# Two MLPs and two attentions on one core: third sweep in groups of two pairs, second attention run without MLP steps inside, low parts of a weight kept in DRAM, a reordered norm chain

## The chip, the cores and the metric

The kernel runs on one core of one Trainium2 chip. The metric is device time of the whole program, from the first to the last instruction and a little around them, as the median of several runs.

## What is computed

A decoder trunk of two layers on one sequence of 1024 tokens, width 1024, all in float32. Layer 0 mixes with an mLSTM in chunks of 128; layer 1 with a causal attention of 8 heads, whose keys and values come from a shared low-rank latent. Each mixer and each MLP stands between two RMS norms:

```python
x = x + g1 * rmsnorm(mixer(modulate(rmsnorm(x, norm_g[l, 0]), sh1, sc1)), norm_g[l, 1])
h = modulate(rmsnorm(x, norm_g[l, 2]), sh2, sc2)
x = x + g2 * rmsnorm(jnp.square(jax.nn.relu(h @ mlp_w1[l])) @ mlp_w2[l], norm_g[l, 3])
```

The shifts, scales and gates come from `silu(c) @ ada_w[l] + ada_b[l]`. The MLP's hidden width is 4096, so `mlp_w1` is 1024 x 4096 and `mlp_w2` 4096 x 1024.

## The kernel before

**Numbers.** A float32 product is made of three matmuls (`mm3`, L244 to L246): every operand is split into a high part (`fp32r`, a cast on ScalarE) and a low part (the difference, on VectorE). A weight of 128 x 1024 is loaded into `raw` (4 buffers), cast to `wh` (L202) and subtracted to `wl` (L203), both in a ring of 8 (`ws`). A weight's `load` stands two steps ahead of its use (`AHEAD`).

**Halves and sweeps.** The sequence is worked on as two halves of 512 tokens, `hfs[0]` and `hfs[1]`. A layer's MLP runs over both in three sweeps. Hidden columns are taken in 16 pairs (p, 16 + p) of 128 columns. Sweep 1 makes the first 16 hidden blocks of half 0, sweep 2 the other 16, and both use seven products for eight (a scheme with sums and differences of the halves' inputs and of weight blocks), whose remainders are kept in DRAM: `m` (sweep 1's partial product), `u` (two sums per pair) and `s` (a weight sum). Sweep 3 (`third`, L1014) makes the hidden blocks of half 1 from `s` and `u`. A sweep is a list of steps: `hid` steps, each 24 matmuls of 128 x 512 (36 in sweep 2) that make hidden blocks, and `out` steps (`up_cols` in layer 0, `up_rows` in layer 1), which multiply the group's hidden blocks by `mlp_w2` into PSUM (`pm`) and add the result to the running sum in SBUF (`accumulate`, the `L211 DVE k<-k,pm` rows). A group is 1, 2 or 4 pairs; the `out` steps of a group follow the `hid` steps of the next one. The second weights are loaded and split again in sweep 3.

After a `hid`'s matmuls come an addition on VectorE, two functions on ScalarE (relu, square; L928, L929), a cast (L457) and a subtraction (L458).

**Two streams.** `two_streams(dense, other, fill)` (L2342) writes the order on TensorE by hand: `other`, a mixer, yields a number n after each piece of work, and n steps of `dense`, the MLP, are put behind it, 0.5 for each stretch that `dense` yields (a `yield "within"` splits a step). `fill` (the `ada` vectors) is advanced beside them. So layer 0's sweep 3 runs beside the first half's latents, attention, output projection and norm (`mixer1(hfs[0], ..)`); layer 1's sweep 1 beside those of the second half (`mixer1(hfs[1], ..)`). Sweep 2 of layer 1 needs what the second half's norm gives (`ops`), so the MLP steps that are left when the attention is done are what TensorE has beside the projection (`wout`), the residual and the norm chain (`post`, L2235). A scheduler then orders every engine's list, TensorE's given order kept, by a model of the times and by priorities (`prompt`, `tc.high_priority`).

**Second attention.** Half 1 attends to all keys: 8 heads, two units each (j = 2, 3) of two 128-query blocks, on 640 to 1024 keys. A unit is: scores (`score_mm`, L1498 to L1504, into both banks of a `pm`), softmax (L1508 maximum, L1509, L1510 exponential, L1511, L1512 scaling), `turned` (transpositions on TensorE, L1614 and L1625, each with a cast and a subtraction) in rounds of four key blocks, and `products`. The loop (`attend`, L1603) does, in each round, the last round's products, the transpositions, after the last round the next unit's scores, then MLP steps by `next(dense)`, here `cycle((0, 0.5))`.

**Norm chain.** `post` scales eight blocks of 128 x 512 by the norm (L2261), then forms from them and from half 0's stored `keep` (`u`) the operands of sweep 2: `ops[2]`, `ops[3]`, later `ops[4]`; `aside` forms `ops[0]` and `ops[1]` for sweep 3. Sweep 2's own weights need five differences on VectorE for each `hid` (L980 to L987, the first result used is `wv`, L985).

## Time and profile before

| | |
|---|---|
| median of 3 runs | 2411.64 us (2410.61 to 2415.65) |
| the profiled execution | 2413.85 us, its span 2412.1 us |
| TensorE (PE) busy | 2286.9 us, 95% of the span |
| weight loads (PEld), VectorE (DVE), ScalarE (ACT) | 78%, 73%, 45% |
| mean granted TensorE clock | 0.978 |
| moved | 448.47 MB, mean 186 GB/s |

PEclk is the granted TensorE clock as a share of full speed. In a group's row stand the line, the engine, the operation, output and inputs by name, shapes, the count, then busy us and the mean in ns, then the idle time before them and what ended it. A wait's row reads: who, waited for whom, us in total, times, the longest.

### The profile page before, as it was taken

Reading aid. Unit: us, or ns where it says so; the run is one execution under the profiler, and the core shown is the slowest. Engines: PE = TensorE matmul, PEld = TensorE weight load, DVE = VectorE, ACT = ScalarE, POOL = GpSimd, SP = SyncE. Lnnn points to the kernel's source line nnn. Section 1 sums busy time; section 2 is a strip of 40 time slices with the busy share of each in tenths; the row PEclk is TensorE's granted clock in tenths of the full one; section 3 lists DMA queues with packets and bytes.
Section 4 is the critical chain, followed back from the end, with each engine's and each line's share of the span. In section 5 each row is a group of like instructions: output and inputs, shape, how many; then the busy total and the mean of one; then the engine's idle time right before and its main releaser. Section 6 shows DMA issues by size and latency. Waiting matters only on the chain. (4 is left out here: it accounts for less than half of the span.)

```text
span 2412.1 us, 31013 instructions
## 1 busy us (share of the span) xinstructions
PE 2286.9 (95%) x11274; PEld 1891.3 (78%) x11274; DVE 1756.6 (73%) x2825; ACT 1075.7 (45%) x1795; POOL 18.3 (1%) x95
## 2 busy tenths in 40 slices
PE   8999999999999889899989999999999699999998
PEld 6888888888778677777878777788877488878887
DVE  6666767799787777788875987766647876666556
ACT  4365336565323245344444465444444333454433
POOL 1000000000000000000000000000000000000000
PEclk9999999999999999999999999999999899999999
DMA  9544555556697875545554664965256487675321
GB/s 316 172 128 123 157 149 164 178 187 207 211 290 224 248 263 167 161 130 176 170 171 146 205 217 150 308 207 183 90 153 206 127 272 234 217 259 196 117 88 70
DMA packets 384186, 448.47 MB, mean 186 GB/s; under 512 B 28867, under 2 KB 258304, under 8 KB 384032
## 3 DMA queue, kind: packets, MB, share of 16 engines
q1 hardware_dynamic: 383744, 446.38, 58.2%
q8 instruction: 89, 1.46, 0.2%
q14 instruction: 65, 0.53, 0.1%
q0 software_dynamic: 288, 0.10, 0.0%
HBM read 341.55 MB, written 104.86 MB: 185 GB/s over the span
## 5 line engine op out<-in xcount | busy, mean ns | idle before, releaser
L202 ACT CAST wh<-raw 128x1024 fp32r<-128x1024 f32 (+2 forms) x339 | 344.3, 1018 | 513.7 <-PE ps L244 119.5
L203 DVE TENSOR_TENSOR wl<-raw,wh 128x1024 fp32r<-128x1024 f32 (+2 forms) x339 | 400.0, 1182 | 223.7 <-ACT wh L202 210.7
L244 PE MATMUL ps<-k,wl 128*128 128x512 f32 x1100 | 437.7, 398 | 9.3 <-DVE wl L203 4.4
L245 PE MATMUL ps<-k,wh 128*128 128x512 f32 x1100 | 432.1, 393 | 2.5 <-DVE k L458 2.4
L246 PE MATMUL ps<-k,wh 128*128 128x512 f32 x1100 | 430.9, 392 | 0.0
L244 PEld LDWEIGHTS ps<-k,wl 128*128 128x128 f32 x1100 | 208.1, 189 | 57.3 <-DVE wl L203 5.4
L245 PEld LDWEIGHTS ps<-k,wh 128*128 128x128 f32 x1100 | 208.3, 189 | 46.9 <-DVE k L458 4.8
L246 PEld LDWEIGHTS ps<-k,wh 128*128 128x128 f32 x1100 | 208.2, 189 | 44.1
L211 DVE TENSOR_TENSOR k<-k,pm 128x512 f32<-128x512 f32 (+1 forms) x234 | 200.7, 884 | 57.0 <-PE pm L246 56.4
L244 PE MATMUL pm<-hd,wl 128*128 128x512 f32 x512 | 205.2, 401 | 5.7 <-DVE k L211 5.7
L245 PE MATMUL pm<-hd,wh 128*128 128x512 f32 x512 | 201.7, 394 | 1.7 <-DVE hd L458 1.7
L246 PE MATMUL pm<-hd,wh 128*128 128x512 f32 x512 | 201.4, 393 | 0.0
L244 PE MATMUL pm<-wh,hd 128*128 128x512 f32 x488 | 193.2, 396 | 6.6 <-DVE hd L458 2.7
L245 PE MATMUL pm<-wl,hd 128*128 128x512 f32 x488 | 190.8, 391 | 0.0
L246 PE MATMUL pm<-wh,hd 128*128 128x512 f32 x488 | 190.8, 391 | 0.0
L348 DVE SCALAR_TENSOR_TENSOR tma<-raw,cond,tma 128x512 f32<-128x512 f32 x168 | 125.7, 748 | 17.5 <-DMA raw<-in_ada_w_dram 9.1
L928 ACT ACTIVATE tmp<-tmp 128x512 f32<-128x512 f32 x80 | 50.5, 631 | 160.6 <-DVE tmp L211 136.2
L244 PEld LDWEIGHTS pm<-hd,wl 128*128 128x128 f32 x512 | 97.7, 191 | 28.4 <-DVE k L211 7.2
L245 PEld LDWEIGHTS pm<-hd,wh 128*128 128x128 f32 x512 | 97.7, 191 | 23.0 <-DVE hd L458 2.6
L244 PEld LDWEIGHTS pm<-wh,hd 128*128 128x128 f32 x488 | 92.0, 189 | 28.3 <-DVE hd L458 3.5
L246 PEld LDWEIGHTS pm<-hd,wh 128*128 128x128 f32 x512 | 97.4, 190 | 20.8
L246 PEld LDWEIGHTS pm<-wh,hd 128*128 128x128 f32 x488 | 92.0, 189 | 19.5
(425 smaller groups left out, 4324.0 us busy)
## 6 DMA issues: line engine op xcount, KB each, us to landing
raw<-in_mlp_w_dram SPq DMA_DIRECT2D x160, 512.0 KB, 4.7
raw<-in_ada_w_dram SPq DMA_DIRECT2D x80, 512.0 KB, 4.5
raw<-in_mlp_w_dram SPq DMA_DIRECT2D x128, 256.0 KB, 4.0
raw<-in_a_w_in_dram SPq DMA_DIRECT2D x44, 512.0 KB, 4.6
s<-k SPq DMA_DIRECT2D x32, 512.0 KB, 3.4
u<-k SPq DMA_DIRECT2D x32, 512.0 KB, 4.2
raw<-s SPq DMA_DIRECT2D x32, 512.0 KB, 3.4
xs<-k SPq DMA_DIRECT2D x40, 256.0 KB, 4.8
```

The source lines that it names most:

```text
L202: nc.scalar.copy(hi[:, :n], r[:, :n])
L203: i = nc.vector.tensor_sub(lo[:, :n], r[:, :n], hi[:, :n].bitcast(F32))
L211: return f(*a, **k)
L244: nc.tensor.matmul(o, ll, rh, start=start, stop=False)
L245: nc.tensor.matmul(o, lh, rl, start=False, stop=False)
L246: pe_last[0] = nc.tensor.matmul(o, lh, rh, start=False, stop=stop)
L348: nc.vector.scalar_tensor_tensor(acc, r[:, kk], cond[:, k : k + 1], acc, ALU.mult, ALU.add)
L928: nc.scalar.activation(s, s, AF.Relu)
```

## The change

- Layer 0's sweep 3 takes groups of two pairs (`[2] * 8` for `[1] * 14 + [2]`), layer 0's sweep 1 and layer 1's sweep 1 groups of four. With `own`, a group's `out` steps follow its own `hid` steps.
- `out` steps multiply the hidden blocks in the order in which they were made, both banks of `pm` side by side.
- In layer 0's sweeps 1 and 2 the low part of each second weight is also stored to DRAM (`lo`); sweep 3 loads it into the `ws` ring and does not subtract.
- `attend` has a branch for the second half: "group" first runs MLP steps to the end of a group, then scores of the next unit stand between a unit's transpositions, and MLP steps stand only behind the whole attention. The first half's MLP step per unit stands in one place.
- `two_streams` counts a step as 1 (or half at "within") and carries a remainder.
- `wout` in the mixers loads two weights ahead; `post` forms the difference of the two halves' blocks before the norm is known (eight scalings on ScalarE), and the rest of the old chain (`rest`) is put into sweep 2's `hid` steps 1 to 4. The yields after the second attention change.

```diff
--- before
+++ after
...
@@ -852,10 +855,16 @@
-    def wout(w, o, store, wide=False):
-
+    def wout(w, o, store, wide=False, ahead=0):
+
+        load = lambda m: wload([(0, 0, wcols(w, m * P))], P)
+        ready = [load(m) for m in range(ahead)]
+        if ahead:
+            yield
         for m in range(KD):
-            pt = proj_fm(w, m * P, o, one_pm if wide and m % 2 else ps)
+            if m + ahead < KD:
+                ready.append(load(m + ahead))
+            pt = proj_of(ready.pop(0), o, one_pm if wide and m % 2 else ps)
@@ -920,6 +929,7 @@
             self.keep = scratch([D, H], f"keep{l}")
+            self.lo = scratch([4, P, DFF // P, 256], f"lo{l}")
@@ -998,6 +1008,8 @@
                 prompt(nc.vector.tensor_add)(u2, u2, pt)
+                if p_ and ops["later"]:
+                    ops["later"].pop(0)()
@@ -1101,15 +1113,20 @@
             def out(ws):
-                for t in range(t0, t1):
-                    if t % 2 == 0:
-                        if t > t0:
-                            yield "within"
-                        b2 = pm()
-                    block(b2[:, t % 2], ws, t)
-                    if t % 2:
+                made = list(hids)
+                for t in range(t0, t1, 2):
+                    if t > t0:
+                        yield "within"
+                    b2 = pm()
+                    for j, q in enumerate(sorted(range(G), key=lambda q: made.index(fs[q]))):
+                        w, (hh, hl) = ws[q // 2], hids[fs[q]]
                         for e in range(2):
-                            self.accumulate((half, t - 1 + e, g), y.t[t - 1 + e][:, g], b2[:, e])
+                            mm3(
+                                b2[:, e], hh[:, ts(t + e, P)], hl[:, ts(t + e, P)],
+                                w[0][:, q % 2], w[1][:, q % 2], j == 0, j == G - 1,
+                            )
+                    for e in range(2):
+                        self.accumulate((half, t + e, g), y.t[t + e][:, g], b2[:, e])
@@ -1118,22 +1135,43 @@
             def out(w):
-                for m in range(i * n, (i + 1) * n):
-                    if m % 2 == 0:
-                        if m > i * n:
-                            yield "within"
-                        b2 = pm()
-                    pt = b2[:, m % 2]
-                    for q, f in enumerate(fs):
-                        c_ = ts(m - i * n, P)
-                        mm3(pt, w[0][:, q, c_], w[1][:, q, c_], *hids[f], q == 0, q == G - 1)
-                    if m % 2:
-                        self.accumulate((half, m), y.t[m // 2], b2)
+                for m in range(i * n, (i + 1) * n, 2):
+                    if m > i * n:
+                        yield "within"
+                    b2, made = pm(), list(hids)
+                    for j, q in enumerate(sorted(range(G), key=lambda q: made.index(fs[q]))):
+                        for e in range(2):
+                            c_ = ts(m + e - i * n, P)
+                            mm3(
+                                b2[:, e], w[0][:, q, c_], w[1][:, q, c_], *hids[fs[q]],
+                                j == 0, j == G - 1,
+                            )
+                    self.accumulate((half, m + 1), y.t[m // 2], b2)
             views = [(a, 0, wcols(w2, i * n * P, n * P, f, r)) for a, f, r in self.runs(fs)]
-            return lambda: wload(views, n * P), out
-
-        def steps(self, half, y, sweep, groups, prev=(), lead=False):
+
+            def load():
+                if not half:
+                    w = wload(views, n * P)
+                    nc.sync.dma_start(self.lo[i][:, fs[0] : fs[0] + G], w[1].bitcast(F32))
+                    return w
+                r = raw()
+                w = [
+                    sb.tile([P, 1024], F32R, tag="ws", bufs=WS, name=f"wk_{next(uid)}").rearrange(
+                        "p (a b) -> p a b", b=n * P
+                    )
+                    for _ in range(2)
+                ]
+                rv = r.rearrange("p (a b) -> p a b", b=n * P)
+                for a, f, k in self.runs(fs):
+                    nc.sync.dma_start(rv[:, a : a + k], wcols(w2, i * n * P, n * P, f, k))
+                    nc.sync.dma_start(w[1][:, a : a + k].bitcast(F32), self.lo[i][:, f : f + k])
+                nc.scalar.copy(w[0], rv)
+                return w
+
+            return prompt(load), out
+
+        def steps(self, half, y, sweep, groups, prev=(), lead=False, own=False):
@@ -1149,6 +1187,8 @@
                 prev = [self.up(half, y, fs, j, sweep == 3 and fs[-1] == 2 * NPR - 1) for j in range(len(fs))]
+                if own:
+                    steps, prev = steps + prev, []
@@ -1162,7 +1202,8 @@
                     yield from f(w)
-                    yield steps[(n - AHEAD + 1) % len(steps)][1].__name__
+                    after = steps[(n - AHEAD + 1) % len(steps)][1].__name__
+                    yield "lead" if (f.__name__, after) == ("out", "hid") else after
@@ -1172,9 +1213,9 @@
-        def sweep1(self, hf, y, sizes):
+        def sweep1(self, hf, y, sizes, own=False):
             g = self.groups(sizes, list, lambda p_: self.first(p_, hf.h2))
-            return self.steps(0, y, 1, g)
+            return self.steps(0, y, 1, g, own=own)
@@ -1196,12 +1237,12 @@
-        def sweep3(self, hf, y, sizes, buf):
+        def sweep3(self, hf, y, sizes, buf, own=False):
             )
-            steps, last = self.steps(1, y, 3, g)
+            steps, last = self.steps(1, y, 3, g, own=own)
@@ -1656,6 +1688,39 @@
+        def score(u, e):
+            st, n = pm(), (2 * u.j + e + 1) * P
+            score_mm(lambda g: st[:, g], hf.kk, u.q, u.kn, 2 * u.j + e)
+            u.prs.append(raw())
+            softmax(st.rearrange("p a b -> p (a b)")[:, :n], u.prs[e], n, e == 0)
+
+        def ahead():
+            for head, j in next(groups, []):
+                u = Half()
+                (u.hh, u.q, u.kn, u.v), u.j, u.nk, u.prs = head, j, 2 * j + 2, []
+                return u
+
+        if hf.i:
+            yield "group"
+            u = ahead()
+            for e in range(2):
+                score(u, e)
+            while u:
+                then, done = ahead(), []
+                for e in range(2):
+                    b0 = 4 * e
+                    work = [(u, b0, min(4, u.nk - b0))]
+                    done.append((work, turned(work)))
+                    if then:
+                        score(then, e)
+                    elif e:
+                        behind()
+                for work in done:
+                    products(*work)
+                yield next(dense)
+                u = then
+            return
+
@@ -1777,7 +1842,7 @@
         yield 0.5
-        yield from attend(hf, units(), cycle((0.5,)), lambda: load_o(hf), 0.5, piece)
+        yield from attend(hf, units(), cycle((1,)), lambda: load_o(hf), 0, piece)
@@ -1802,7 +1867,7 @@
-        yield from attend(hf, units(), cycle((0, 0.5)), lambda: load_o(hf))
+        yield from attend(hf, units(), cycle((0,)), lambda: load_o(hf))
@@ -2243,7 +2308,12 @@
                 )
-            u = FH(tiles=u)
+            u, d = FH(tiles=u), [k4v(), k4v()]
+            d = [d[k // 2][:, k % 2] for k in range(4)]
+            for k in range(4):
+                for j in (k, 4 + k):
+                    nc.scalar.activation(y[j], y[j], AF.Identity, scale=A[:, j : j + 1])
+                nc.vector.tensor_sub(d[k], y[4 + k], y[k])
@@ -2252,28 +2322,31 @@
         ops = hf.ops
-        ops[2], ops[3] = half_op(), half_op()
-        ts2 = []
+        ops[2] = half_op()
+        b1, b2 = ([sh[:, j : j + 1] for j in range(i, i + 4)] for i in (0, 4))
+        for k in range(4):
+            with tc.high_priority(PRIO):
+                nc.vector.tensor_mul(d[k], d[k], rstd)
+                nc.vector.scalar_tensor_tensor(d[k], d[k], b2[k], u[k], ALU.add, ALU.add)
+                split_mod(ops[2].hi[k], ops[2].lo[k], d[k], None)
+            yield waits[4]
+        ops[3] = half_op()
             with paced():
-                y1, y2, b = y[k], y[4 + k], sh[:, 4 + k : 5 + k]
-                for j in (k, 4 + k):
-                    nc.vector.scalar_tensor_tensor(
-                        y[j], y[j], A[:, j : j + 1], rstd, ALU.mult, ALU.mult
-                    )
-                nc.vector.tensor_sub(y1, y1, u[k])
                 t = tmc()
-                nc.vector.scalar_tensor_tensor(t, y2, b, y1, ALU.add, ALU.subtract)
-                split_mod(ops[2].hi[k], ops[2].lo[k], t, None)
-                ts2.append(t)
-            yield waits[4]
-        for k, t in enumerate(ts2):
-            with paced():
-                b1, b = sh[:, k : k + 1], sh[:, 4 + k : 5 + k]
-                nc.vector.scalar_tensor_tensor(u[k], t, b1, u[k], ALU.subtract, ALU.subtract)
-                split_mod(ops[3].hi[k], ops[3].lo[k], u[k], None)
-                nc.vector.scalar_tensor_tensor(u[4 + k], u[4 + k], b, t, ALU.add, ALU.subtract)
+                nc.vector.scalar_tensor_tensor(t, d[k], b1[k], u[k], ALU.subtract, ALU.subtract)
+                split_mod(ops[3].hi[k], ops[3].lo[k], t, None)
+                nc.vector.scalar_tensor_tensor(
+                    u[4 + k], u[4 + k], b2[k], d[k], ALU.add, ALU.subtract
+                )
             yield waits[5]
+
+        def rest(k):
+            nc.vector.tensor_mul(y[k], y[k], rstd)
+            nc.vector.tensor_sub(y[k], y[k], u[k])
+            nc.vector.tensor_mul(y[4 + k], y[4 + k], rstd)
+
+        ops["later"] = [lambda k=k: rest(k) for k in range(4)]
@@ -2343,7 +2416,7 @@
         traced = nc.cur_bb.bb.instructions
-        at, per = ["hid"], 0
+        at, per, due = "hid", 0, 0
@@ -2351,15 +2424,18 @@
                 per, n = more, 0
-            while n == "align" and at[0] != "hid" or n != "align" and n > 0:
-                at[0] = go(dense)
-                if at[0] is end:
+            whole = n in ("align", "group")
+            if not whole:
+                due = due + n if n else 0
+            while at not in ("lead", n == "align" and "hid") if whole else due > 0:
+                was, at = at, go(dense)
+                if at is end:
                 pace[0] = next(i for i in reversed(traced) if i.engine == dve)
-                if at[0] != "within":
+                if at != "within":
                     some(fill, per)
-                if n != "align":
-                    n -= 0.5
+                if not whole:
+                    due -= 0.5 if "within" in (was, at) else 1
@@ -2400,7 +2476,7 @@
-    steps, tail = ms[0].sweep1(hfs[0], z0, [4, 4, 4, 2, 2])
+    steps, tail = ms[0].sweep1(hfs[0], z0, [4] * 4)
@@ -2423,17 +2499,24 @@
         y = FH(claim=True)
+        last = wout(b_w_out[0], hf.o, lambda m, pt: evac(y[m], pt), ahead=2)
+        next(last)
         yield 1
-        yield "align"
-        for _ in wout(b_w_out[0], hf.o, lambda m, pt: evac(y[m], pt)):
+        if not hf.i:
+            yield "align"
+        for _ in last:
         yield from post(
-            hf, y, B2, x_cols, A3, adac(1, SH2), ms[1], ((3, 3, 3, 5, 1), (2, 1, 1, 4, 0.5, 0))[hf.i]
+            hf, y, B2, x_cols, A3, adac(1, SH2), ms[1], ((3, 3, 3, 5, 1), (2, 2, 2, 3, 0.5, 0.5))[hf.i]
+    turn_of = cycle((0, 1))
+
+        if next(turn_of):
+            return tmc(), tmp()
@@ -2442,12 +2525,12 @@
     two_streams(
-        ms[0].run(ms[0].sweep3(hfs[1], z1, [1] * 14 + [2], pair_buf)),
+        ms[0].run(ms[0].sweep3(hfs[1], z1, [2] * 8, pair_buf, True)),
     u0 = FH(claim=True)
-    steps, tail = ms[1].sweep1(hfs[0], u0, [2] * 8)
+    steps, tail = ms[1].sweep1(hfs[0], u0, [4] * 4, True)
...
```

`proj_of` multiplies a loaded weight as `proj_fm` did; the first half's `scores` keeps the shape for j < 2 alone.

More of the change, by code (lines that the diff above doesn't have):

```diff
@@ L1519, in scores @@
         prs = []
[L1520 to L1536 removed]
+        st = pm()
+        pr = raw().rearrange("p (a b) -> p a b", b=512)
+        for e in range(2):
+            score_mm(lambda g: st[:, e], kk, q, kn, 2 * j + e)
+        for e in range(2):
+            n = (2 * j + e + 1) * P
+            softmax(st[:, e, :n], pr[:, e], n, e == 0)
+            prs.append(pr[:, e])
         return prs
@@ L1657, in begin @@
             return us
+        def score(u, e):
[11 more added lines that the diff above has]
+            u = ahead()
+            for e in range(2):
+                score(u, e)
+            while u:
+                then, done = ahead(), []
+                for e in range(2):
+                    b0 = 4 * e
[10 more added lines that the diff above has]
+            return
         late = None
```

22 lines of the change are left out of this document (3 added, 19 removed).

## The prediction

> **What bounds the kernel now.** I read the busy time by stage first (VectorE is DVE, ScalarE ACT, TensorE PE, its weight loads PEld), then who PE waits for, then the chain that ended last at the worst place.
>
> ```profile
> core 0: us, PE busy (x) PEld busy (x) DVE busy (x) ACT busy (x) POOL busy (x), PEclk, DMA share, GB/s
> 0.00:445.00 445.00, 434.49 (x2693) 365.79 (x2694) 307.67 (x617) 208.22 (x422) 9.27 (x43) 1.00 0.56 172
> 445.00:640.00 195.00, 193.27 (x852) 158.23 (x851) 165.22 (x234) 107.70 (x152) 0.00 (x0) 1.00 0.63 199
> 640.00:880.00 240.00, 215.51 (x917) 174.29 (x916) 197.14 (x299) 78.21 (x110) 0.39 (x4) 0.96 0.81 250
> 880.00:1355.00 475.00, 443.08 (x2103) 364.99 (x2102) 361.98 (x578) 211.23 (x363) 4.04 (x20) 0.96 0.54 170
> 1355.00:1555.00 200.00, 186.45 (x806) 150.55 (x805) 160.48 (x228) 106.11 (x168) 0.76 (x5) 0.96 0.64 207
> 1555.00:1757.00 202.00, 195.51 (x1172) 169.46 (x1171) 136.46 (x239) 94.70 (x173) 3.23 (x17) 0.99 0.51 173
> 1757.00:1880.00 123.00, 119.51 (x521) 98.39 (x522) 76.27 (x104) 51.98 (x74) 0.20 (x2) 0.97 0.55 171
> 1880.00:1930.00 50.00, 26.98 (x106) 20.05 (x105) 44.76 (x71) 15.69 (x24) 0.00 (x0) 0.83 0.46 138
> 1930.00:2115.00 185.00, 185.00 (x837) 152.49 (x836) 124.13 (x181) 71.98 (x102) 0.39 (x4) 1.00 0.76 238
> 2115.00:2412.10 297.10, 287.13 (x1280) 237.09 (x1279) 182.45 (x282) 129.83 (x210) 0.00 (x0) 0.99 0.44 146
> ```
>
> The stages are: layer 0's mixer (to 445), its sweeps 1 and 2 (to 640 and 880), sweep 3 beside the first attention (to 1355), layer 1's sweep 1 beside latent work (to 1555), beside the second attention (to 1757), and beside output projection and norm (to 1930), then layer 1's sweeps 2 and 3. PE is the bound throughout. The change removes no matmul, so all it can win is PE idleness (stage length less PE busy) and half-rate clock (stage times one less PEclk). In 880:1355 that is 31.9 us idle and 19 us of clock, 51 together. In 640:880 it is 24.5 and 10; in 1757:1930, 26.5 and 12 (partly the same moments).
>
> The Trainium skill (Perfetto Trace Analysis, Identifying the Most-Contended Engine) calls matmul occupancy a poor measure of headroom and wants weight-load occupancy instead. In 880:1355 that would leave 110 us. The trace disagrees here: in 1930:2115 PE is never idle and PEld is still 82%.
>
> The timeline gives PE's pace; PE's waits and the busy time around the longest of them follow.
>
> ```profile
> 2300.74 0.39 PE L244 MATMUL ps<-k,wl 128*128 128x512 f32 x1
> ...
> 2305.50 0.39 PE L244 MATMUL ps<-k,wl 128*128 128x512 f32 x1
> ```
>
> These two rows are 21 matmuls apart: 0.227 us each, so an MLP step of 24 matmuls takes 5.45 us.
>
> ```profile
> PE ps L244 <- DVE wv L985: 18.8, 1, 18.8
> ```
>
> ```profile
> 1889.40:1908.20 18.80, 0.04 (x2) 0.03 (x1) 18.80 (x32) 6.78 (x11) 0.00 (x0) 0.64 0.02 10
> 1908.20:1912.00 3.80, 3.80 (x9) 3.00 (x10) 2.79 (x3) 2.66 (x5) 0.00 (x0) 0.53 0.99 294
> ```
>
> PE stood 18.8 us while DVE was busy in every one of them, and afterwards ran at about half rate.
>
> **The change, part by part.** I count savings as negative.
>
> *A, norm chain and cover of layer 1 (1757:1930).*
>
> ```profile
> 1877.35 3.40 DVE k L2261 x5
> ...
> 1907.52 0.60 DVE wv L985
> ```
>
> From the norm's result (1877.35) to the first `wv` (1907.52) DVE ran 30.2 us, 48 instructions by the chain's rows between these, 0.63 us each. In the changed program DVE's order has 56 there: the combination moves ahead of the norm, but the scheduler pulls eight products and four differences of the deferred `rest` forward into this stretch. That is 35 us, 5 more. PE's order, on the other hand, has five MLP steps after the norm's sum matmul instead of three, 10.9 us more cover. The 18.8 us would shrink to about 13; the longer yields before it (2, 2, 2, 3 for 2, 1, 1, 4) should take the other 7.7 us of idleness, and some clock. I take -12. If DVE eats the cover, 0; if everything goes, 26.5 and a little clock, -28.
>
> *B, second attention without MLP steps (1555:1757).*
>
> ```profile
> L458 DVE TENSOR_TENSOR hd<-pc,hd 128x512 fp32r<-128x512 f32 x47 | 31.8, 687 | 7.1 <-ACT hd L457 4.7 <-PE ps L245 1.7 <-issue 0.5
> ...
> L1508 DVE TENSOR_REDUCE sm<-pm 128x1 f32<-128x1024 f32 x7 | 8.5, 1220 | 2.1 <-PE pm L1504 2.1
> ...
> L1512 DVE TENSOR_SCALAR raw<-raw,sm 128x1024 f32<-128x1024 f32 x7 | 5.3, 752 | 0.2
> ...
> L1511 DVE RECIPROCAL sm<-sm 128x1 f32<-128x1 f32 x28 | 4.5, 162 | 15.4 <-ACT raw L1510 14.8
> ...
> L1509 DVE TENSOR_SCALAR sm<-sm 128x1 f32<-128x1 f32 x28 | 4.2, 150 | 0.5
> ```
>
> On ACT, and four of a unit's transpositions twice over in the chain:
>
> ```profile
> L1510 ACT ACTIVATE raw<-pm,sm 128x1024 f32<-128x1024 f32 x7 | 7.8, 1121 | 12.2 <-DVE sm L1509 12.2
> ...
> L1510 ACT ACTIVATION_READ_ACCUMULATOR raw<-pm,sm 128x1 f32 x28 | 5.4, 194 | 0.0
> ```
>
> ```profile
> 1742.13 0.87 PE pc L1614 x8
> ```
>
> The steps are moved, not removed: the code now runs whole groups until two of the four are done before the attention, and has 15 steps' worth of yields after it. Inside, PE's cover must come from the next unit's scores. A unit (two 128-query blocks of a head; 16 units) has a softmax chain after its last score of 1.22 + 0.15 + 1.12 + 0.19 + 0.16 + 0.75 = 3.6 us at 1024 keys. PE's order in the changed program puts between that score and the first transposition that needs it the products, 18 or 24 matmuls of 256 columns (half of 0.227 each: 2.0 to 2.7 us), and before the second transposition ten score matmuls more (about 2 us): 4 us or more. DVE has about 6.2 us a unit: 3.5 splits at 0.687, and two maxima and scalings at 832 keys on average, 1.98 and 1.22 by scaling the 1024-key rows, and 0.62 of single columns. PE has about 7.8: two times five score matmuls over 832 columns (3.7), 14 transpositions at 0.109 (1.5), 21 products (2.4), and the mask's. So the chain is just covered, with nothing to spare. I take 0.4 us a unit, +6. Bounds: with no cover at all the whole chain stands bare, 16 x 3.6 = +58, which is a rival below; the range for the covered case is -6 (all of the 6.5 us idle now) to +32 (2 us a unit).
>
> *C, sweep 3 in groups of two pairs, low parts from DRAM (880:1355).*
>
> ```profile
> L203 DVE TENSOR_TENSOR wl<-raw,wh 128x1024 fp32r<-128x1024 f32 x50 | 61.1, 1223 | 41.2 <-ACT wh L202 41.0
> L211 DVE TENSOR_TENSOR k<-k,pm 128x1024 f32<-128x1024 f32 x49 | 59.7, 1219 | 18.4 <-PE pm L246 18.2
> ```
>
> Fifteen groups become eight, each with four accumulations: 28 fewer at 1.219 us, 34 us. The 32 second weights need no subtraction: 39 us at 1.223. DVE falls from 362 to about 289 us, 76% to 61%. A relieved neighbour shows what is left at that load: in 1757:1880 (DVE 62%) PE loses 3.5 us idle and 3.7 of clock in 123 us, 5.9%; on 475 us that is 28 instead of 51, -23. In 1555:1757 (DVE 68%) it loses 6.5 and 2.0 us in 202, 4.2%, which would give -31. I take -26, between them. Ends: -8 if the waits are for something other than DVE load, -45 if nearly all go. Reading 16.8 MB of low parts raises 0.54 DMA share by 35 GB/s on 170, which stays low.
>
> *D, layer 1's sweep 1 in four groups.* 32 fewer accumulations of 128x512, on PE's path only where DVE is behind (1355:1555, 80% DVE, 13.5 us idle). I take -5, between -12 and 0.
>
> *E, writing the low parts (445:880).*
>
> ```profile
> DMA packets 59947, 60.11 MB, mean 250 GB/s; under 512 B 6337, under 2 KB 49356, under 8 KB 59935
> ...
> s<-k SPq DMA_DIRECT2D x16, 512.0 KB, 3.1
> ```
>
> ```profile
> SPq L1005 <- DVE k L211: 29.3, 8, 8.3
> ```
>
> These rows are of 640:880. Twenty of the 32 stores of 512 KB fall in it (sweep 2's sixteen, and the four of sweep 1's last group, which run with it): 10.5 MB on 60.1, 294 GB/s, close to the 294 of the 3.8 us row above at a 0.99 share. Each also waits in SP's queue for a DVE subtraction, as the `u` store (L1005) does, and the raw loads of later weights queue behind it. Cost between 0 and 34 us (20 x 1.7, 512 KB at 300 GB/s, all exposed); I take +5, since PE has covered the similar `s` stores mostly.
>
> *F, small ones.* `rest` and the eight scalings on ACT add twelve DVE instructions to layer 0's sweep 2 too, 8 us at 0.63, hidden where DVE has room: +2 (0 to 8). Two output weights loaded ahead: -2 (-3 to 0). The sorted order of the outs hides the newest hidden block behind the older three (18 matmuls, 4.1 us): nothing; if DVE and ACT lag, it is inside C's bounds.
>
> Sum: -12 + 6 - 26 - 5 + 5 + 2 - 2 = -32. The profiled execution took 2413.85 us (1.75 around the span), so 2381.9; the median is 2.2 below the profiled one: 2380.
>
> **Rivals.**
> - *Bare attention (slower).* DVE and ACT work through their lists in order, and one late split delays the maximum of the next block, so the cover counted in B doesn't work: +58 instead of +6 gives +20, 2432; if every unit also loses a half-rate stretch like the 3.8 us one, 1.7 us more, 2459. It decides from 2.4 us a unit (38/16). For it: the chain is as long as its cover. Against: 4 us of cover by PE's order, and DVE at 6.2 of 7.8 us. By the Trainium skill (TensorE: Matmul & The Clock Gate, Part 1) the clock halves only after an idle window of about 3.4 us, so short waits alone would not bring 2459; the 18.8 us row agrees, and no row here shows short waits in series.
> - *Transfers bind layer 0.* E at +34 and F at +8 instead of 5 and 2: +3, 2415. For it: 0.81 share and SP's waits. Against: slots free in 445:640.
> - *Sweep 3's idleness is not DVE load.* C at -8: 2398. For it: several of its waits are single dependencies. Against: 76% DVE beside attention.
> - *All of the cover pays.* C -45, A -28, B -4: 2335.
>
> That the scheduler puts MLP steps back into the attention is excluded by PE's order.
>
> **How the numbers follow.** Forecast 0.46 (own range 2364 to 2396), bare attention 0.12, transfers 0.09, sweep 3 unmoved 0.19, all pays 0.14. Range 2334 to 2412: it holds all but bare attention and some of the transfers and of the lowest case. About 0.2% is what a measurement of this kernel can tell from no change. Slower: 0.12 and half of transfers, 0.17; same 0.03; faster 0.80.
>
> **What would show it.** After: DVE down by 73 us in sweep 3 and PE idle there near 15; `wv`'s wait at the second norm about 13; PE's waits for the softmax's scaling under 1 us each in a second attention without MLP matmuls. Wrong: PE waiting 2.4 us or more per unit for the softmax; DMA waits of `raw` grown by 20 us in layer 0's sweep 2; sweep 3's idleness unchanged with DVE at 61%.

## The result, and the profile after

| | before | changed |
|---|---|---|
| median | 2413.13 us (2410.61 to 2415.65, 4 runs) | 2393.39 us (2390.72 to 2397.70, 4 runs) |
| ratio, 95% interval | | 0.992 (0.9899 to 0.9941) |
| profiled execution, span | 2413.85, 2412.1 us | 2390.72, 2388.9 us |

The changed kernel is 20 us faster (23 by the profiled executions); the sum had given 32. Its profile begins:

```profile
PE 2281.3 (95%) x11274; PEld 1886.1 (79%) x11274; DVE 1675.5 (70%) x2745; ACT 1085.7 (45%) x1811; POOL 17.6 (1%) x95
...
L203 DVE TENSOR_TENSOR wl<-raw,wh 128x1024 fp32r<-128x1024 f32 (+4 forms) x307 | 360.9, 1178 | 220.8 <-ACT wh L202 198.8
...
L211 DVE TENSOR_TENSOR k<-k,pm 128x512 f32<-128x512 f32 (+1 forms) x170 | 141.3, 859 | 69.5 <-PE pm L246 69.3
```

The matmuls are as many as before (11274). The subtractions are 32 fewer (339 before), the accumulations 64 fewer (234 before), and DVE is busy 81 us less (1756.6 before).

Stages begin and end at other times now, so they are compared at equal work: each matmul record counts by its columns at the full-rate pace (0.227 us for 512, 0.109 for a transposition), which gives the same sum in every kernel here, and a stage runs from one amount of started work to another. The four stages of the argument are sweep 3 with the first attention, the second half's latents, the second attention, and projection with norm. Before:

```profile
core 0: us, PE busy (x) PEld busy (x) DVE busy (x) ACT busy (x) POOL busy (x), PEclk, DMA share, GB/s
874.60:1399.70 525.10, 489.57 (x2293) 402.32 (x2292) 408.24 (x639) 237.32 (x402) 4.83 (x28) 0.96 0.53 169
1399.70:1542.90 143.20, 133.35 (x589) 108.00 (x588) 110.73 (x160) 78.05 (x127) 0.00 (x0) 0.96 0.68 221
1542.90:1758.10 215.20, 207.83 (x1226) 179.43 (x1225) 146.44 (x255) 99.47 (x181) 3.60 (x18) 0.99 0.53 181
1758.10:1944.20 186.10, 160.38 (x690) 129.81 (x689) 130.97 (x187) 75.47 (x109) 0.20 (x2) 0.94 0.55 171
```

The changed kernel, same columns:

```profile
877.60:1378.40 500.80, 479.73 (x2295) 396.70 (x2293) 338.57 (x575) 236.10 (x399) 4.31 (x28) 0.98 0.67 216
1378.40:1523.40 145.00, 132.56 (x588) 107.16 (x587) 111.58 (x162) 76.58 (x124) 0.00 (x0) 0.96 0.63 206
1523.40:1749.70 226.30, 211.75 (x1239) 179.31 (x1238) 142.22 (x248) 105.22 (x186) 3.67 (x20) 1.00 0.55 187
1749.70:1921.70 172.00, 158.68 (x677) 128.33 (x676) 123.49 (x176) 80.77 (x118) 0.00 (x0) 0.96 0.55 174
```

The second column is the length. Sweep 3 is 24.3 us shorter: DVE has 70 us less work in it, PE's idleness fell from 35.5 us to 21.1 and the clock's part (length times one less PEclk) from 21 to 10. The second attention is 11.1 longer at less DVE work: 14.6 us idle where 7.4 were (7 of the 11; the other 4 are in PE's busy time, 211.75 for 207.83, and what they are stays open). Projection and norm are 14.1 shorter. PE's waits for a `pc` buffer in the attention before (the transpositions are L1614 there), its waits in the changed kernel's attention, and those from there to sweep 2:

```profile
PE pc L1614 <- DVE hd L458: 2.1, 2, 1.8
PE pc L1614 <- DVE raw L1512: 1.8, 4, 1.0
```

```profile
PE pc L1646 <- DVE hd L458: 7.6, 10, 1.6
PE ps L244 <- ACT hd L457: 1.7, 7, 0.2
...
PE pc L1646 <- DVE raw L1553: 1.0, 1, 1.0
```

```profile
PE pm L244 <- DVE hd L458: 7.7, 1, 7.7
PE ps L244 <- DVE wv L995: 4.1, 1, 4.1
PE ps L245 <- DVE k L458: 1.5, 4, 0.8
```

In the attention PE waits for splits (L458) of earlier transpositions, 7.6 us where it was 2.1, and hardly for the softmax's scaling (L1553, 1.0 us in all). One such wait in the timelines of DVE and then of PE:

```profile
1640.44 0.96 DVE L1549 TENSOR_REDUCE sm<-pm 128x1 f32<-128x768 f32 x1
1641.31 0.58 DVE L1553 TENSOR_SCALAR raw<-raw,sm 128x640 f32<-128x640 f32 x1
...
1641.87 1.27 DVE L458 TENSOR_TENSOR hd<-pc,hd 128x512 fp32r<-128x512 f32 x2
```

```profile
1642.60 0.66 PE L1646 MATMUL pc<-ident,raw 128*128 128x128 f32 x4 [0.70 <-DVE hd L458]
```

The first of these splits ends near 1642.5, behind a maximum and a scaling in DVE's list, and PE's next transpositions (1642.60), which need its `pc` buffer, begin then. At the norm the one wait of 18.8 us has become two, 4.1 for `wv` and 7.7 for the last hidden block's split. DVE's list during the latter:

```profile
1850.53 2.49 DVE L2329 TENSOR_TENSOR k<-k,tmc 128x512 f32<-128x512 f32 x4
1852.93 0.69 DVE L2345 TENSOR_TENSOR k<-k,tmc 128x512 f32<-128x512 f32 x1
1853.54 0.69 DVE L2347 TENSOR_TENSOR k<-k,tmc 128x512 f32<-128x512 f32 x1
...
1858.28 0.69 DVE L2347 TENSOR_TENSOR k<-k,tmc 128x512 f32<-128x512 f32 x1
1858.88 2.08 DVE L2330 SCALAR_TENSOR_TENSOR k<-k,ada,hd 128x512 f32<-128x512 f32 x3
1860.87 0.69 DVE L458 TENSOR_TENSOR hd<-tmp,hd 128x512 fp32r<-128x512 f32 x1
```

Eight products of the deferred `rest` (L2345, L2347) and the norm chain (L2329, L2330) stand ahead of the split (1860.87) for which PE waits.

### The profile page after: what moved, and what is told of

It is laid out like the page before. It is cut to its first block, busy times and chain, and to the rows that moved or that the text cites. A ratio compares the mean times of both kernels' runs of the same rounds, so it can differ in the third digit from the quotient of the medians.

```text
span 2388.9 us, 31122 instructions
## 1 busy us (share of the span) xinstructions
PE 2281.3 (95%) x11274; PEld 1886.1 (79%) x11274; DVE 1675.5 (70%) x2745; ACT 1085.7 (45%) x1811; POOL 17.6 (1%) x95
## 4 chain that ended last, share of the span: by engine, by line
PE 73%; DVE 12%; DMA 9%; ACT 3%; issue 2%; SPq 1%; DVEq 0%; ACTq 0%
PE ps L244 12%; PE ps L245 12%; PE ps L246 12%; PE pm L244 8%; PE pm L245 8%; PE pm L246 8%; DMA raw<-in_mlp_w_dram 4%; DVE wl L203 2%; PE pc L245 2%; PE pc L244 2%; PE pc L246 2%; DVE k L211 1%; ACT wh L202 1%; DVE hd L458 1%; DVE tma L348 1%
## 5 line engine op out<-in xcount | busy, mean ns | idle before, releaser
L202 ACT CAST wh<-raw 128x1024 fp32r<-128x1024 f32 (+4 forms) x307 | 310.5, 1014 | 471.6 <-PE pm L245 119.8
L203 DVE TENSOR_TENSOR wl<-raw,wh 128x1024 fp32r<-128x1024 f32 (+4 forms) x307 | 360.9, 1178 | 220.8 <-ACT wh L202 198.8
L244 PE MATMUL ps<-k,wl 128*128 128x512 f32 x1100 | 436.7, 397 | 12.8 <-DVE wl L203 5.8
L246 PE MATMUL ps<-k,wh 128*128 128x512 f32 x1100 | 430.5, 391 | 0.0
L244 PEld LDWEIGHTS ps<-k,wl 128*128 128x128 f32 x1100 | 207.9, 189 | 61.6 <-DVE wl L203 7.3
L246 PEld LDWEIGHTS ps<-k,wh 128*128 128x128 f32 x1100 | 207.6, 189 | 43.8
L244 PE MATMUL pm<-wh,hd 128*128 128x512 f32 x488 | 192.3, 394 | 9.8 <-DVE hd L458 8.9
L246 PE MATMUL pm<-wh,hd 128*128 128x512 f32 x488 | 190.7, 391 | 0.0
L211 DVE TENSOR_TENSOR k<-k,pm 128x512 f32<-128x512 f32 (+1 forms) x170 | 141.3, 859 | 69.5 <-PE pm L246 69.3
L244 PEld LDWEIGHTS pm<-wh,hd 128*128 128x128 f32 x488 | 92.1, 189 | 30.5 <-DVE hd L458 9.7
L246 PEld LDWEIGHTS pm<-wh,hd 128*128 128x128 f32 x488 | 92.1, 189 | 19.3
L245 PEld LDWEIGHTS pm<-wl,hd 128*128 128x128 f32 x488 | 92.2, 189 | 19.1 <-issue 0.2
L244 PE MATMUL pm<-hd,wk 128*128 128x512 f32 x256 | 102.1, 399 | 0.3 <-ACT hd L457 0.3
L245 PE MATMUL pm<-hd,wk 128*128 128x512 f32 x256 | 100.6, 393 | 1.2 <-DVE hd L458 1.2
L246 PE MATMUL pm<-hd,wk 128*128 128x512 f32 x256 | 100.1, 391 | 0.0
L244 PE MATMUL pm<-hd,wl 128*128 128x512 f32 x256 | 99.8, 391 | 0.0
L245 PE MATMUL pm<-hd,wh 128*128 128x512 f32 x256 | 99.7, 389 | 0.0
```

Of the source, the lines that this page charges most:

```text
L202: nc.scalar.copy(hi[:, :n], r[:, :n])
L203: i = nc.vector.tensor_sub(lo[:, :n], r[:, :n], hi[:, :n].bitcast(F32))
L211: return f(*a, **k)
L244: nc.tensor.matmul(o, ll, rh, start=start, stop=False)
L245: nc.tensor.matmul(o, lh, rl, start=False, stop=False)
L246: pe_last[0] = nc.tensor.matmul(o, lh, rh, start=False, stop=stop)
```

## The experiments

Twelve kernels ran, in four groups with runs of before beside them (its medians there 2412.2 to 2413.1). In the table, a stage's entry is its change of length against before at equal work, in us, from the profiled execution; the first stage is layer 0's sweeps 1 and 2. "Cover" is the number of weight matmuls (L244 to L246) that PE's records hold between the second half's last norm sum and the first use of `wv`; 24 are an MLP step.

| kernel | median us | sweeps 1, 2 | sweep 3 | latents | attention | norm | cover |
|---|---|---|---|---|---|---|---|
| changed | 2393.4 | +3.2 | -24.3 | +1.8 | +11.1 | -14.1 | 120 |
| 1 no low parts kept | 2402.9 | +2.2 | -14.8 | +2.1 | +11.1 | -13.9 | 120 |
| 2 tiny stores, subtraction kept | 2400.2 | +3.0 | -13.1 | +2.9 | +11.0 | -12.9 | 120 |
| 3 `rest` late | 2387.6 | +1.7 | -24.9 | +1.4 | +10.6 | -15.3 | 120 |
| 4 old attention | 2395.2 | +1.1 | -28.5 | +7.0 | +1.2 | +1.3 | 72 |
| 5 old groups in sweep 3 | 2396.5 | +3.5 | -15.8 | -3.8 | +12.1 | -13.9 | 120 |
| 6 old norm chain | 2390.1 | +3.7 | -23.4 | +4.2 | +10.5 | -16.7 | 120 |
| 7 = 3 and 4 | 2392.1 | +2.4 | -24.9 | +5.0 | +0.2 | 0.0 | 72 |
| 8 layer 1 in eight groups, `own` | 2411.0 | +2.4 | -28.8 | +8.0 | +12.3 | +0.3 | 216 |
| 9 layer 1 in the old eight groups | 2383.1 | +1.7 | -25.2 | +6.9 | +10.2 | -21.2 | 264 |
| 10 = 3 with other yields | 2385.0 | +1.6 | -25.6 | +1.5 | +10.5 | -15.0 | 120 |
| 11 attention begun mid-group | 2400.0 | +0.9 | -29.0 | +1.4 | +25.0 | -15.8 | 264 |
| 12 = 3 and 9 | 2377.4 | +1.6 | -25.5 | +4.4 | +10.0 | -25.6 | 264 |

What one profile is worth shows in sweep 3's column: ten of the kernels have the same code there, and lie between -23.4 and -29.0. A stage difference under 3 us from one profile means nothing by itself.

**1, no low parts kept.** `return lambda: wload(views, n * P), out` in `up_cols`, as before: no stores, sweep 3 subtracts.

> The changed kernel without the stored low parts: sweep 3 subtracts them again (32 subtractions of 1.22 us on DVE, 39 us), nothing is written in sweeps 1 and 2. Theory A (the relief of DVE is what pays in sweep 3, the stores cost transfers in sweeps 1 and 2): sweeps 1 and 2 are 8 to 10 us shorter than with the stores, sweep 3 about half of its 29 us gain longer, 12 to 18; in all 2395 to 2402, slower than the changed kernel by 3 to 9 us. Rival B (the gain of sweep 3 is from the fewer accumulations and the order of the steps, the subtractions were hidden anyway): sweep 3 within 4 us of the changed kernel, in all 2383 to 2388, faster than it.

Measured 2402.94 (ratio to before 0.996, 0.9948 to 0.9972), 9.5 us over the changed kernel. Sweeps 1 and 2 are no shorter without the stores (+2.2 against +3.2), and sweep 3 gives up 9.5 of its 24.3. So theory A has the direction, but neither of its sizes: nothing for the stores, and less than 12 to 18 in sweep 3.

**2, the stores' size.** The stores stay, of 8 columns each; sweep 3 subtracts.

```diff
-                    nc.sync.dma_start(self.lo[i][:, fs[0] : fs[0] + G], w[1].bitcast(F32))
+                    nc.sync.dma_start(self.lo[i][:, fs[0], 0:8], w[1][:, 0, 0:8].bitcast(F32))
```

> As the kernel without stored low parts, but each low part still sends 8 of its 1024 columns to DRAM: SP waits for the subtraction as before, hardly a byte is moved; sweep 3 subtracts again. Theory A1 (the stores cost bandwidth): sweeps 1 and 2 as without any store, within 2 us. Rival A2 (SP's queue is held by the wait for the subtraction, and the loads behind it come late): sweeps 1 and 2 as long as in the changed kernel, 8 to 10 us longer than without a store.

Measured 2400.24 (0.9954, 0.9942 to 0.9966). Sweeps 1 and 2 at +3.0: with full stores, tiny ones or none they last the same. Neither the 16.8 MB nor the places in SP's queue cost what a profile can show.

**3, `rest` late.** All twelve of layer 1's deferred instructions are tied behind sweep 2's first addition.

```diff
-                prompt(nc.vector.tensor_add)(u2, u2, pt)
-                if p_ and ops["later"]:
+                added = prompt(nc.vector.tensor_add)(u2, u2, pt)
+                if self.rows:
+                    while ops["later"]:
+                        with tc.issue_after(added.ins):
+                            ops["later"].pop(0)()
+                elif p_ and ops["later"]:
```

> The changed kernel with the twelve deferred norm instructions of layer 1 tied behind the first addition of sweep 2, so that they no longer stand before the first wv on DVE. Theory C (the DVE list before the first wv sets when sweep 2 begins): the two waits of the changed kernel there, 7.7 us for a hidden block's split and 4.1 us for wv, shrink to 4 us or less together, 7 to 9 us gained with some clock, 2383 to 2387. Rival D (they are hidden behind the MLP steps, what PE waits for is the loads of keep or of the weights): within 2 us of the changed kernel.

Measured 2387.60 (0.9893, 0.9879 to 0.9906), 5.8 us under the changed kernel. Its waits from the attention's end to sweep 2:

```profile
PE ps L244 <- DVE wv L995: 4.1, 1, 4.1
PE ps L245 <- DVE k L458: 4.0, 1, 4.0
PE pm L244 <- DVE hd L458: 2.9, 1, 2.9
```

The wait for the last split fell from 7.7 to 2.9, the one for `wv` did not move, and the one for `k` grew from 1.5 to 4.0. So the pulled-forward products stood before the split and not before `wv`, as neither reading had it. In this profile the norm's stage is only 1.2 us shorter, and the intervals of the two kernels overlap; that the products cost about 5 us is likely, not shown.

**4, the old second attention.** The branch `if hf.i:` in `attend` is off, the yields are those of before (`cycle((0, 0.5))`; 2, 1, 1, 4, 0.5, 0), layer 1's sweep 1 has its old groups; the new norm chain stays.

> The changed kernel with the second half's attention as it was before: MLP steps inside (0 and 0.5 in turn), sweep 1 of layer 1 in groups of one pair less (eight groups of two), the old yields of the norm chain; the rest as changed. Theory E (the bare attention costs 9 us, the steps saved for the norm chain win 12.5): 2393 to 2400, 0 to 6 us slower than the changed kernel. Rival F (the shorter norm chain alone makes the 12.5 us, the moved attention is a loss): 2381 to 2386, faster than the changed kernel by 7 to 12 us.

Measured 2395.22 (0.9926, 0.9915 to 0.9938). That is theory E's range. The attention is 10 us shorter than in the changed kernel, the norm 15 longer, and the latents 5. The wait at the norm:

```profile
PE ps L244 <- DVE wv L995: 15.4, 1, 15.4
PE pm L244 <- DVE k L211: 6.7, 2, 5.0
PE pm L244 <- DVE hd L458: 2.6, 1, 2.6
```

With 72 matmuls of cover the new chain leaves 15.4 of the old one's 18.8, and the stage gains nothing.

**5, old groups in sweep 3.** `[1] * 14 + [2]` without `own`, low parts from DRAM (which lie there in another order, so that groups of one pair can read them).

> The changed kernel, but layer 0's sweep 3 keeps the old groups (fourteen of one pair and one of two, sixty accumulations); the low parts still come from DRAM. With the run that has the new groups and no stored low parts (9.5 us slower than the changed kernel), this splits term C in two. Theory additive: the two reliefs of VectorE add up, so this kernel lies above the changed one (2393) by what is left of sweep 3's gain, 12 to 15 us: 2405 to 2408, with PE about 12 us more behind at the end of sweep 3. Rival, one relief is enough: with the 39 us of subtractions gone VectorE has room, and the 28 accumulations cost little: 2394 to 2398. Rival, the order of the groups is what pays (each group's outs directly behind its hids), whatever VectorE does: 2410 or more.

Measured 2396.54 (0.9926, 0.991 to 0.9942), 3.1 over the changed kernel. Sweep 3's rows of runs 1 and 5:

```profile
877.60:1387.90 510.30, 483.95 (x2294) 400.81 (x2292) 373.34 (x606) 236.49 (x399) 4.71 (x28) 0.97 0.55 173
```

```profile
879.90:1389.20 509.30, 480.80 (x2293) 395.10 (x2293) 373.66 (x608) 236.76 (x401) 4.28 (x28) 0.98 0.66 211
```

DVE has 408 us of work before, 373 with either relief, 339 with both; the stage is 15 us shorter with either and 24 with both. So within the stage most of both reliefs is kept. By its median run 5 lies in the range of the second reading, but not for its reason: without the accumulations' relief sweep 3 is 8.5 us longer. The kernel loses only 3 in the end, since its latents are 3.8 shorter than before, the changed kernel's 1.8 longer. A wait stands there that is short in run 5; first the changed kernel, then run 5, from 1375 to 1455 us:

```profile
PE ps L244 <- ACT k L457: 4.2, 1, 4.2
PE pc L448 <- DVE tmc L444: 2.4, 1, 2.4
PE ps L245 <- DVE k L458: 2.2, 1, 2.2
```

```profile
PE ps L244 <- DVE tmp L211: 4.5, 1, 4.5
PE ps L244 <- ACT k L457: 0.4, 1, 0.4
```

So with the new groups in sweep 3 about 6 us are lost again in the latents. It does not go by how much sweep 3 gained: runs 1 and 2, with the new groups and 15 and 13 us gained, have latents of +2.1 and +2.9 too. Why, no run tells.

**6, the old norm chain** in both layers, with the new attention and yields.

> The changed kernel with the norm chain of the kernel before in both layers (A applied after the norm's sum, no deferred products); the waits 2, 2, 2, 3, 0.5, 0.5 of layer 1 and the attention stay. It splits term A into chain and cover. By the prediction's steps the cover (five MLP steps instead of three, 10.9 us) does the work and the pulled-forward products take 5 us of it back: without the new chain 0 to 5 us faster, 2388 to 2393. Rival, the shorter chain does the work: the 18.8 us wait comes back less 10.9 of cover, about 8 in the place of 4.1, and other waits behind it, 2397 to 2402.

Measured 2390.12 (0.9901, 0.9886 to 0.9917), 3.3 faster than the changed kernel, the intervals overlapping; the first reading's range.

```profile
PE ps L244 <- DVE wv L995: 10.9, 1, 10.9
...
PE pm L244 <- DVE hd L458: 0.4, 1, 0.4
```

One wait of 10.9 in the place of 4.1 and 7.7. With 18.8 (neither), 15.4 (chain alone) and 10.9 (cover alone) the two by two is complete: the chain brings 3.4 of `wv`'s wait with the old cover, 6.8 with the new one, and there it puts as much (7.7 for 0.4) in front of the last split.

**7, runs 3 and 4 together.**

> The old second attention with MLP steps inside, with the old waits and sweep 1 of layer 1 (that run alone: 1.8 us above the changed kernel), together with layer 1's deferred products tied behind sweep 2's first accumulation (that run alone: 5.8 us below it). Theory independent: 2393.4 + 1.8 - 5.8 = 2389. Rival, the deferred products are bare where cover is short: with three steps of cover the 15.4 us wait at the norm loses all of the eight products and four differences, 12 x 0.63 = 7.6 us, and its slow clock behind it, 2384 to 2387, which would beat every run so far. Rival, the wait is then ended by something else: 2393 or more.

Measured 2392.13 (0.9903, 0.9886 to 0.9919): 3.1 under run 4, the intervals overlapping, and between the first reading (2389) and the third (2393 or more). `wv` is waited for 14.9 us (15.4 without): the deferred products stand behind it, not before it, and the second reading falls.

**8, layer 1 in eight groups with `own`.** `[2] * 8, True` for `[4] * 4, True`.

> The changed kernel with layer 1's sweep 1 in eight groups of two pairs instead of four of four pairs, each group's outs still directly behind its hids. It brings back 32 accumulations of 128 x 512 and measures term D by itself. The prediction's D: 5 us slower than the changed kernel, 2398 (0 to 12). Rival, they are covered: 2392 to 2395.

Measured 2411.03 (0.9991, 0.9981 to 1.0): 17.6 us slower than the changed kernel, which neither reading had. From the attention's end to sweep 2:

```profile
PE pm L244 <- DVE hd L458: 21.6, 7, 10.1
```

With `own`, a group's `out` steps need the hidden block just made; in a group of two pairs less other work stands between, and beside the projection and the norm DVE is late with that split.

**9, layer 1 in its old eight groups.** `[2] * 8`, without `own`.

> The changed kernel with layer 1's sweep 1 as in the kernel before: eight groups of two pairs, the outs of a group between the hids of the next. It brings back the 32 accumulations of term D, but not what made the run with eight groups and the outs directly behind their own hids 17.6 us slower. Theory, the 17.6 us were the newest hidden block's split laid bare: PE no longer stands 25 us for L458 here, and the result is the changed kernel's plus term D, 2393 to 2398. Rival, eight groups start the attention earlier or later in the MLP steps and that is what costs: 2405 or more here too.

Measured 2383.13 (0.9876, 0.9855 to 0.9897): 10.3 us faster than the changed kernel, below both readings. From the attention's end to sweep 2:

```profile
PE pc L448 <- DVE tmc L444: 3.4, 1, 3.4
PE pm L244 <- DVE k L211: 3.3, 5, 1.0
PE pm L244 <- DVE hd L458: 1.1, 1, 1.1
```

No wait for `wv` is left, and without `own` run 8's 21.6 us are 1.1. The table's last column says why `wv` is ready: "group" stops at the next group's end, which comes sooner with small groups, so the attention begins earlier and 264 matmuls (eleven steps), not 120 (five), stand behind the norm's sum. By the profiles run 9 is 7.2 us faster than the changed kernel: the norm is 7.1 shorter, the latents are 5.1 longer, and the rest is spread over the other stages, under 3 us in each. So the cover accounts for the norm, but not by itself for the 10.3.

**10, more yields behind the sum.** Run 3 with 2, 1, 1, 5, 0.5, 0.5 for 2, 2, 2, 3, 0.5, 0.5.

> The run with layer 1's deferred products tied behind sweep 2's first accumulation (2387.6), with layer 1's waits 2, 1, 1, 5, 0.5, 0.5 in the place of 2, 2, 2, 3, 0.5, 0.5: two MLP steps more after the norm's sum, two fewer before it. Theory, cover after the sum is what counts: the waits of 4.1 for wv and 2.9 for the last hidden block go, 3 to 7 us faster, 2381 to 2385. Rival, the two steps are missed before the sum, where the accumulated sums of squares wait for VectorE: 2388 to 2395.

Measured 2384.96 (0.9884, 0.9867 to 0.99), 2.6 under run 3, the intervals overlapping. `wv`'s wait is still 4.1 and the cover still 120: sweep 1 has no steps left to give, whatever the yields ask. The time lies in the first reading's range, but its mechanism did not take place.

**11, the attention begun mid-group.** `yield "align"` for `yield "group"`: four groups, with the attention and the cover at the places of run 9 (the 267 of the expectation are 264 and a few others).

> The changed kernel with layer 1's four groups of four pairs, but the bare attention starts at the next hid step instead of at the next group boundary. By PE's order this puts 267 matmuls between the second norm's sum and the first weight wv, instead of 120, exactly as in the run with layer 1's old eight groups (2383.1), and the attention stands at the same place in the order as there. So two things are told apart. First, theory that the steps left for the norm made that run 10 us faster: 2376 to 2385 here, with no wait for wv; rival, the old groups themselves did: 2391 to 2395. Second, term D by itself is the difference of this run to that one: by the prediction's -5, 2378; rival, the 32 accumulations are covered: 2383; rival, groups of four pairs cost: 2386 or more.

Measured 2399.98 (0.9947, 0.9929 to 0.9965), 6.6 slower than the changed kernel. `wv` is not waited for, but the output projection behind the attention is (its wait, then PE's timeline, then ACT's):

```profile
PE ps L244 <- DVE wl L203: 9.7, 5, 1.9
```

```profile
1741.56 0.50 PE L244 MATMUL ps<-k,wl 128*128 128x512 f32 x1 [1.94 <-DVE wl L203]
...
1742.94 0.63 PE L246 MATMUL ps<-k,wh 128*128 128x512 f32 x1
1743.36 0.63 PE L244 MATMUL ps<-k,wl 128*128 128x512 f32 x1
```

```profile
1748.50 1.05 ACT L202 CAST wh<-raw 128x1024 fp32r<-128x1024 f32 x1 [7.11 <-PE ps L244]
```

Each of five weights is cast only when PE has done with the one before it: the ring of eight has no place free. The weights of four-pair `out` steps, loaded ahead and waiting for the attention's end, are likely in it; that is argued from the code. So the run was meant to isolate term D and does not. It does show that 264 matmuls of cover alone do not make the kernel faster.

**12, runs 3 and 9 together.**

> The run with layer 1's old eight groups (2383.1) with layer 1's deferred products tied behind sweep 2's first accumulation (5.8 us faster in the changed kernel). Theory independent: 2377, the fastest so far. Rival: with 267 matmuls of cover the deferred products are hidden anyway, 2381 to 2385; rival, tied behind the first accumulation they come later into sweep 2 than its reader wants, and cost: over 2386.

Measured 2377.41 (2374.70 to 2380.86; 0.9853, 0.9834 to 0.9871): the fastest of all, 16.0 us under the changed kernel. The time is the first reading's (2377 expected), though the intervals of runs 9 and 12 overlap.

## Why the prediction was right, and where not

The direction was right, the forecast's case came true (2393.4 lies in its own range of 2364 to 2396), and the terms C and A held. B and E were mis-sized, and D did not show in its stage. The time alone would not decide it: 2393.4 is nearer to the 2398 of the rival in which sweep 3's idleness is not DVE load than to the sum's 2380. What decides is that sweep 3 gave 24.3 us and not 8.

- **C, sweep 3 (-26).** -24.3; over the ten profiles with this code -26.0 on average. DVE lost 70 us (73 forecast) and PE 14 us of idleness (17 forecast, from 31.9 to near 15 between narrower bounds). Runs 1, 2 and 5 bear out that it is DVE's load, as argued: two different edits that each take 35 us off DVE bring 13 to 16. The rival in which sweep 3's waits are for something else is out.
- **A, norm (-12).** -14.1, and by the cover: 120 matmuls for 72 are the five steps for three. The chain by itself brought nothing (run 6 is as fast without it, run 4's stage gains nothing from it). "Shrink to about 13" was 4.1 and 7.7 together, 11.8. The scheduler did pull the products forward, but they stood before the last hidden block's split, not before `wv`. Put late, they make the kernel 3 to 6 us faster in three pairs (changed and 3, 4 and 7, 9 and 12), near the 5 put down for them, though in each pair the intervals overlap.
- **B, attention (+6).** +11.1, and 10.5 to 12.1 in the six other kernels that have it at the same place with the same groups: the term was sized at 0.4 us a unit and is 0.7. Of the 11.1 us the wait for splits grew by 5.5, and about 4 stay open. The softmax chain was covered, as worked out. What was left out is the ring of two `pc` buffers: a unit's later transpositions wait until VectorE has split the earlier ones, and there the splits stand behind maxima and scalings in its list. The sum compared the chain with its cover and not DVE's order with the buffers. That more buffers would mend it was not tried. The rival's mechanism lay near, with its order turned round: it had a late split delay a maximum in DVE's list, and the row shown has a maximum and a scaling delay a split. At 0.7 us a unit it is far from the 2.4 us from which it would have decided.
- **D, layer 1's groups (-5).** In the latents, four groups cost +1.4 on average over eight kernels, the old eight +5.8 over four (4, 7, 9, 12): -4.4, near its size. But it was counted against the latents of before, and there it shows in run 5 alone (-3.8), whose sweep 3 has the old groups; beside the new ones something that stays open costs the stage about 6. And the prediction was wrong in that this was all that the groups do. Large groups with "group" also push the attention back by up to a group and leave 120 matmuls for the norm, where run 9 leaves 264 and its norm is 7.1 shorter; with the old groups the kernel is 10 us faster. In the sum that belonged to A, whose cover was counted in PE's order but never compared with what other groups would leave.
- **E, the stores (+5).** Nothing beyond the noise of a profile: runs 1 and 2. The rival in which transfers bind layer 0 is out, though the share there rose from 0.81 to 0.87.
- **F.** Sweeps 1 and 2 are longer by 1 to 4 us in every kernel, with stores or without. That is near the +2 put down, but not for the reason given: run 6, which has none of the deferred instructions, shows +3.7. The output weights loaded ahead were not tried by themselves.

The profiled execution was forecast at 2381.9 and took 2390.7. Of these 8.8 us, 6.8 are the latents (+1.8 for -5), 5.1 the attention (+11.1 for +6) and 1.7 sweep 3; the norm gives 2.1 back and sweeps 1 and 2 3.8 (+3.2 for +7); the rest, about 1, includes the -2 of the output weights, which shows in no stage. So that the whole came within 9 us is in part luck: 13.6 us missed in three places stand against 5.9 won in others.

## What to carry to other kernels

When work is moved out of one stage to cover another, count what the second stage has left in the order, in matmuls, and ask what decides that number: here a rule about where a group ends was worth more than the shorter chain. Relief of a secondary engine pays where TensorE waits for it often and briefly, and can be sized from a neighbouring stage at the load that it will have. Before calling a dependency covered, lay the buffers that it passes through against the order of the engine that frees them, not only its latency against the cover.

## What the runs showed of the hardware

Short waits can cost the clock, by where they fall. In run 11 PE stood 1.94 us before each of five weights. These are stretches of 3.41 us there, laid where the granted clock changes. Behind a stretch's length stands PE's busy time; the third number from the end is the granted clock:

```profile
1739.28:1742.69 3.41, 1.47 (x7) 0.95 (x6) 1.84 (x2) 2.08 (x3) 0.00 (x0) 1.00 0.04 5
1742.69:1746.10 3.41, 3.41 (x10) 2.64 (x9) 0.00 (x0) 0.00 (x0) 0.00 (x0) 0.50 0.44 149
1746.10:1749.51 3.41, 2.82 (x13) 1.98 (x11) 0.00 (x0) 1.01 (x2) 0.00 (x0) 1.00 0.00 0
1749.51:1752.93 3.42, 2.07 (x9) 1.72 (x10) 1.84 (x2) 1.15 (x3) 0.00 (x0) 1.00 0.17 37
1752.93:1756.34 3.41, 3.41 (x17) 2.71 (x15) 0.00 (x0) 0.14 (x1) 0.00 (x0) 1.00 0.39 117
```

The wait that ended at 1741.56 lay whole within the first stretch and left 1.47 us of it busy; in the next one the clock was 0.50, and matmuls came 0.43 us apart (the rows at 1742.94 and 1743.36). The following wait, as long, fell across two stretches, which kept 2.82 and 2.07 us, and the clock stayed at 1.00. So it went on: the first, third and fifth wait were each followed by a slow stretch, the second and fourth were not. In all fourteen profiles the slow stretches begin on one such grid per run. From 40 us on, a stretch at full clock that was followed by half clock had at most 2.0 us busy (three had 2.5), and one that was not had at least 1.47.

The prediction had leaned on the Trainium skill (TensorE: Matmul & The Clock Gate, Part 1), by which the clock falls after an idle window of about 3.4 us; here 1.94 us of idleness inside one stretch of 3.41 us were enough. In the second attention of the changed kernel, with waits of at most 1.6 us, the clock stayed at 1.00.
